# A two-layer streaming encoder on one core: early store of one residual block, accumulating last stores, four more weight blocks split by VectorE, and a longer lead for DMAs

## The chip, the cores and the metric

The kernel runs on one core of a Trainium2 chip, in one launch, and is timed in device microseconds (us). The engines work side by side: PE multiplies matrices, PEld loads its weights, DVE (VectorE) and ACT (ScalarE) work element by element, POOL (GpSimd) helps and issues DMAs, SP (SyncE) only issues DMAs. Each engine runs its own instructions in a fixed order and waits on semaphores. DMAs are issued by SP and ACT (hardware queues, with eight semaphore lanes DMAHW0 to DMAHW7 between them) and by POOL (software queue, lanes DMASW0 to DMASW7). An issue that reuses a lane waits, in its engine's order, until the lane's last DMA has landed. DMAs that add to what lies at their destination ("accumulating") are issued by POOL here.

## The reference

512 frames of 1024 features go through two layers, all in float32. Layer 0 is a convolution module and an MLP; layer 1 is latent attention and an MLP.

```python
def conformer_conv(h, w_pw1, b_pw1, w_dw, b_dw, ln_g, ln_b, w_pw2, b_pw2):
    u = h @ w_pw1 + b_pw1
    a, gate = jnp.split(u, 2, axis=-1)
    u = a * jax.nn.sigmoid(gate)
    ...  # 31 taps along time, each channel by itself, + b_dw
    u = jax.nn.silu(layer_norm(u, ln_g, ln_b))
    return u @ w_pw2 + b_pw2

def squared_relu_mlp(h, w1, w2):
    return jnp.square(jax.nn.relu(h @ w1)) @ w2

def reference(x, ...):
    h = x
    for layer in range(DEPTH):
        ...
        m = conformer_conv(...) if layer < N_A_LAYERS else mla_attention(...)
        h = h + rms_norm(m, mix_post_g[layer])
        f = squared_relu_mlp(rms_norm(h, ffn_pre_g[layer]), w_ff1[layer], w_ff2[layer])
        h = h + rms_norm(f, ffn_post_g[layer])
    return h
```

## The kernel before

**Products in three terms.** A float32 operand is kept as a higher part, which PE multiplies in one pass, and a lower part, the rest. A product is hi·hi + lo·hi + hi·lo, three matmuls (`products_of`, from line 772). A block of weights is 128 x 1024 numbers, 512 KB, and gives 24 matmuls of 512 columns. `weight` (731 to 766) fetches a block into a tile `raw` by SP and makes its parts `wh` and `wl` in one of two ways, decided by the condition in line 754:

- by `split` (789): ACT copies `raw` to `wh`, and VectorE subtracts, `wl = raw − wh`, each in two halves of 512 columns;
- or by DMA: ACT writes −`raw` rounded into `wl` and `raw` into `wh`, two copies each, and POOL issues an accumulating DMA of the whole block from DRAM onto `wl` (512 KB).

`lo_by_dma` (88) names the blocks that may go the second way; the blocks of `pw1`, the convolution's first product, are among them, save the first four (`i >= 4`).

**The convolution.** `pw1` has 16 blocks; column c of 8 (128 features) needs block c and its gate, block 8 + c. The blocks are used in pairs, so blocks 4 to 7 are those of columns c=2 and c=3. Columns 0, 1 and 3 have their 31 taps done by VectorE (`taps_vector`). Columns 2, 4, 5, 6 and 7 have them done by PE (`taps_tensor`, 1160) with 72 small matmuls of `uu` against tap weights that SP loads (`big<-cw`, 256 KB each). For these, `deal_tokens` (1151) sends the gated column through DRAM: ACT issues the store `dealt<-big` and four loads `uu<-dealt` of 64 KB. A layer norm follows, then `pw2` and the rest.

**The end.** `feed_forward(1, ...)` gives the last product by token block b = 0 to 3 (128 frames each) and half dh. `post_norm` (1063) calls `residual` (905) for each: ACT squares F and sums it into `stat`, VectorE multiplies F by a gain row. When both halves of a block are there, VectorE works out the scale rho in a chain of small operations on `stat`, and `finish` (1562) has VectorE add: h = F·rho + h. SP stores the first half, ACT the second, 256 KB each.

**What sets the order.** Nearly all instructions are recorded by `Program` and put in order by a planner in the kernel's own Python (`schedule`), which repeats its plan 16 times with new due times. PE's instructions keep the recorded order except for delays, and the planner puts filler matmuls (`mm<-ident`) where it expects PE to stand still. On the other engines the next instruction is the ready one with the earliest rank; a `dma_start` isn't placed earlier than `LEAD` nanoseconds ahead of its rank (line 251; used in 548). All instructions are issued in line 640, so the rows of the profile are told apart by the names of tiles: `raw`, `wh`, `wl` for weights, `big` and `tmp` for data and tap weights, `uu` and `dealt` for dealt columns, `mm` for PE's results, `h` for the residual stream, `row` for gains.

Of the kernel before, what the change touches and what calls it, by code (L numbers as in the profile page):

```python
# [11 lines left out]
ALU = mybir.AluOpType  # L12
# [10 lines left out]
DH = 512  # L23
# [64 lines left out]
def lo_by_dma(name):  # L88
    if name[0] == "ff1":
        return name[2] == 0 and name[3] < 4  # L90
    if name[0] == "ff2":
        return name[1] == 0 and name[2] == 3 and name[3] in LAST_BY_DMA
    return name[0] in ("pw1", "pw2")
# [152 lines left out]
GAIN_ON = ("vector",)  # L246
# [1 line left out]

PORT = ("tensor_tensor", "scalar_tensor_tensor")

LEAD = 16000.0

BESIDE = 3000.0

# [29 lines left out]
class Program:  # L284
# [166 lines left out]
    def schedule(self, tags):  # L451
# [71 lines left out]
        while left:  # L523
# [19 lines left out]
            while avail[e]:  # L543
# [3 lines left out]
                way = next(w for w in o.ways if w[0] == e)  # L547
                if way[1] == "dma_start" and o.rank > now + LEAD:

                    heappush(future[e], (o.rank - LEAD, o.n, o))  # L550
                    continue
# [92 lines left out]
def trunk(ctx: ExitStack, tc: tile.TileContext, xT, xN, wts, vec, along, rope, cw, out):  # L644
# [3 lines left out]
    nc = Program(tc.nc)  # L648
# [6 lines left out]
    def one(name, shape):  # L655
        return nc.tile(tag(name, 1, shape))
# [13 lines left out]
    def big(dt=F32):  # L670
        return nc.tile(BIG, dt)
# [24 lines left out]
    for k in range(KT):  # L696
        nc.sync.dma_start(out=xf[k], in_=xT[k])

    h = [one(f"h{b}", [P, D]) for b in range(TB)]
# [3 lines left out]
        out=ident, in_=ident, compare_op=ALU.not_equal, fill=1.0, base=0, pattern=[[-1, P]], channel_multiplier=1  # L703
# [13 lines left out]
    def scaled(name, src):  # L717

        lo, hi = ([big(F32R) for _ in range(2)] for _ in range(2))
        for o in range(2):  # L720
            raw = big()
            nc.sync.dma_start(out=raw, in_=src[:, o * T : (o + 1) * T])
            g0 = VEC[GAINS[name[0]]] + 4 * o
            gain = vt[:, g0 : g0 + 4].rearrange("p (k o) -> p k o", o=1).to_broadcast([P, 4, P])
            nc.vector.tensor_tensor(
                out=raw.rearrange("p (k m) -> p k m", m=P), in0=raw.rearrange("p (k m) -> p k m", m=P), in1=gain, op=ALU.mult
            )
            split(raw, slice(0, T), (hi[o], lo[o]))
        return hi, lo

    def weight(key):

        while key not in blocks:
            name, parts = USE[len(blocks)]
            i, n = BLK[parts[0][0]], _cols[BLK[parts[0][0]]]
            if name[0] in GAINS:
                blocks[name] = scaled(name, wts[i])
                continue
            raw, hi, lo = nc.tile(RAW), nc.tile(WH, F32R), nc.tile(WL, F32R)
            step = 256 if i < 2 else n  # L740
            for o in range(0, n, step):
                nc.sync.dma_start(out=raw[:, o : o + step], in_=wts[i, :, o : o + step])
            for other, sign in parts[1:]:
                if sign > 0:
                    nc.gpsimd.dma_start(out=raw, in_=wts[BLK[other]], accum_op=ALU.add)
                else:
                    second = nc.tile(RAW)
                    nc.sync.dma_start(out=second, in_=wts[BLK[other]])
                    for o in range(0, n, 512):
                        nc.vector.tensor_tensor(  # L750
                            out=raw[:, o : o + 512], in0=raw[:, o : o + 512], in1=second[:, o : o + 512], op=ALU.subtract
                        )
            src = raw if len(parts) > 1 else wts[i]
            if i >= 4 and lo_by_dma(name):

                for o in range(0, n, 512):
                    for dst, scale in ((lo, -1.0), (hi, 1.0)):
                        nc.scalar.activation(dst[:, o : o + 512], raw[:, o : o + 512], AF.Copy, scale=scale)
                nc.gpsimd.dma_start(out=lo, in_=src, accum_op=ALU.add)
            else:  # L760
                step = 256 if i < 2 else min(n, 512)
                engines = VG if name[0] in ATT else ("vector",)
                for o in range(0, n, step):
                    split(raw, slice(o, o + step), (hi, lo), engines=engines)
            blocks[name] = hi, lo
        return blocks[key]
# [22 lines left out]
    def split(src, s, dst, d=None, engines=("vector",)):  # L789

        d = s if d is None else d
        nc.scalar.activation(dst[0][:, d], src[:, s], AF.Copy)
        nc.binary(engines, out=dst[1][:, d], in0=src[:, s], in1=dst[0][:, d].bitcast(F32), op=ALU.subtract)
# [77 lines left out]
    def row(name):  # L871
        t = nc.tile(ROW)
        nc.early = 30000.0
        nc.sync.dma_start(out=t, in_=along[ROWS.index(name)])
        nc.early = 0.0
        return t
# [28 lines left out]
    def residual(F, g, b, dh, o, st, on, r2):  # L905


        nc.scalar.activation(
            JUNK, F[b][dh], AF.Square, scale=1.0 / 32 if r2 is None else r2[:, b : b + 1], accum_out=st[:, o : o + 1]
        )  # L910
        nc.binary(on, out=F[b][dh], in0=F[b][dh], in1=g[:, dh * DH : (dh + 1) * DH], op=ALU.mult)

    def rms(st, nb=2, factor=None):

        var = st[:, :nb]
        ss = st[:, 16 : 16 + 2 * nb].rearrange("p (b d) -> p b d", d=2)
        nc.vector.scalar_tensor_tensor(
            out=var, in0=ss[:, :, 0], scalar=RMS_EPS, in1=ss[:, :, 1], op0=ALU.add, op1=ALU.add
        )
        return rsqrt_tiny(st, var, nb, factor)  # L920

    def add_norm(F, rho, bs):

        for i, b in enumerate(bs):
            for dh in range(2):
                cs = slice(dh * DH, (dh + 1) * DH)
                nc.vector.scalar_tensor_tensor(
                    out=h[b][:, cs], in0=F[b][dh], scalar=rho[:, i : i + 1], in1=h[b][:, cs], op0=ALU.mult, op1=ALU.add
                )
                yield b, cs  # L930
# [30 lines left out]
    def feed_forward(layer, X, F):  # L961
# [6 lines left out]
        for q in range(4):  # L968
# [29 lines left out]
            def sides(q, p):  # L998
                return [weight(("ff2", layer, q, p, u)) for u in range(2)]
# [60 lines left out]
                                    op=ALU.add if dests[to] > 0 else ALU.subtract,  # L1060
                                )

    def post_norm(gen, F, g, then, groups, r2=None, last=False):

        group = {b: bs for bs in groups for b in bs}
        seen, st = dict.fromkeys(groups, 0), {}
        for b, dh in gen:
            bs = group[b]
            if not seen[bs]:
                st[bs] = nc.tile(STAT)  # L1070
            if last:

                nc.early = (4000.0, 4000.0, 0.0, 0.0)[b]
            residual(F, g, b, dh, 16 + 2 * (b - bs[0]) + dh, st[bs], GAIN_ON, r2)
            seen[bs] += 1
            if seen[bs] == 2 * len(bs):
                then(bs, rms(st[bs], len(bs), None if r2 is None else r2[:, bs[0] : bs[-1] + 1]))
            nc.early = 0.0

    PAIRS = HALVES[HA], HALVES[HB]  # L1080
    SINGLES = tuple((b,) for b in range(TB))
# [161 lines left out]
    acc, last = big(), LN_ORDER[-1]  # L1243
# [15 lines left out]
    for t0, n in (HA, HB):  # L1259
# [3 lines left out]
        st = nc.tile(STAT)  # L1263
# [5 lines left out]
            out=var, in0=sm[:, nb : 2 * nb], scalar=LN_EPS, in1=d2, op0=ALU.add, op1=ALU.subtract  # L1269
# [20 lines left out]
    def mixer_out(layer, gen):  # L1290

        MF, r2 = token_blocks(), one(f"r2_{layer}", [P, TB])
        Xn = [pair() for _ in range(KT)]

        def on_half(t):
            y, bs = prenorm(Xn, f"ffn_pre{layer}", t), HALVES[t]
            nc.vector.scalar_tensor_tensor(
                out=r2[:, bs[0] : bs[1] + 1], in0=y, scalar=1.0 / 32, in1=y, op0=ALU.mult, op1=ALU.mult
            )

        post_norm(gen(MF), MF, row(f"mix_post{layer}"), by_halves(MF, on_half), PAIRS)
        return Xn, r2

    Xn, r2 = mixer_out(0, pw2)
# [4 lines left out]
    F, r1 = [[None, None] for _ in range(TB)], big()  # L1309
# [4 lines left out]
    def on_half(t):  # L1314
        r1t[t] = prenorm(XH, None, t, r1)

        for b in HALVES[t]:
            nc.sync.dma_start(out=order.rearrange("(m r) d -> r m d", r=R)[b], in_=h[b])

    post_norm(feed_forward(0, Xn, F), F, row("ffn_post0"), by_halves(F, on_half), PAIRS, r2)  # L1320


# [5 lines left out]
    def undealt(a, t):  # L1328

        r0 = t[0] // M  # L1330
        return natural(a)[:, r0 : r0 + t[1] // M]
# [82 lines left out]
    for t in (HA, HB):  # L1414
# [4 lines left out]
        for j in range(2):  # L1419
            rows = slice(64 * j, 64 * j + 64)  # L1420
            nc.vector.tensor_tensor(
                out=undealt(KL[j][rows], t), in0=kr[rows], in1=undealt(KR[rows], t).bitcast(F32), op=ALU.subtract
# [8 lines left out]
    st = nc.tile(STAT)  # L1431
# [127 lines left out]
    Xn, r2 = mixer_out(1, wo)  # L1559
    F = [[None, None] for _ in range(TB)]  # L1560

    def finish(bs, rho):
        for b, cs in add_norm(F, rho, bs):
            (nc.sync, nc.scalar)[cs.start > 0].dma_start(out=out[b, :, cs], in_=h[b][:, cs])

    post_norm(feed_forward(1, Xn, F), F, row("ffn_post1"), finish, SINGLES, r2, last=True)

    with tc.manual_schedule():
        nc.run(tags)
# [126 lines left out]
```

## Time and profile before

| | us |
|---|---|
| median of 3 runs (lowest, highest) | 1066.44 (1065.2, 1067.63) |
| the profiled execution | 1068.46 |
| its span, first to last instruction | 1066.7 |
| mean granted clock of PE, as a share of full speed | 0.993 |
| POOL busy | 141.6 (13%) |
| DMA, share of 16 engines: hardware queue q1, software queue q0 | 40.9%, 25.6% |

Rows of a timeline give start, length, engine, operation, output and inputs, how many instructions are drawn together, and in brackets the idle time of the engine before them and what ended it. ACTq and SPq are DMA issues of these engines. Rows of a tile's view give the issue time of its DMAs and, in a row of its own, how long after the issue they landed. A window gives the busy time of each engine in a stretch, in the order PE, PEld, DVE, ACT, POOL, then the granted clock, the share of time that the DMA engines were busy, and GB/s. A group's row gives the count, the busy time and the mean length of one in ns, and then idle time.

### The profile page before, as it was taken

The page shows a single profiled execution, that of the slowest core. Times are in us where ns is not written, and L with a number is a line of the kernel's source. Part 1 is how long each engine was busy: PE and PEld are TensorE (multiplying, and loading weights), DVE is VectorE, ACT ScalarE, POOL GpSimd, SP SyncE. Part 2 cuts the span into 40 slices and gives each one's busy share as a digit, 9 for nine tenths or more (in the row PEclk, how much of TensorE's full clock was granted, in tenths as well). Part 3 has the DMA queues.
Part 4 walks back from the last instruction along what each step waited for, and adds up shares of the span by engine and source line. Part 5 has one row for each costly group of instructions (what it writes and reads, how often), then busy time and mean ns, then how long its engine had stood idle before and what let it go on. Part 6 is the DMA issues. An engine that isn't in the chain of part 4 may idle for free. (4 is left out here: it accounts for less than half of the span.)

```text
span 1066.7 us, 15181 instructions
## 1 busy us (share of the span) xinstructions
PE 1045.5 (98%) x5284; PEld 884.7 (83%) x5284; DVE 764.1 (72%) x1559; ACT 640.9 (60%) x1343; POOL 141.6 (13%) x165
## 2 busy tenths in 40 slices
PE   8989999999999999999999999999999999999996
PEld 7878988988888888888888888889888888888885
DVE  6497994857438737959988987547574495497698
ACT  8543497766545446545767877558565554454652
POOL 1110011100100100001104533301010010000010
PEclk9989999999999999999999999999999999999998
DMA  9995888657866848658923132557599388485684
GB/s 288 300 254 171 287 211 236 156 168 207 253 171 190 257 126 241 189 182 227 237 69 93 56 100 81 174 182 179 161 245 253 112 235 257 143 243 168 187 237 129
DMA packets 67613, 204.08 MB, mean 191 GB/s; under 512 B 7632, under 2 KB 13904, under 8 KB 67536
## 3 DMA queue, kind: packets, MB, share of 16 engines
q1 hardware_dynamic: 49680, 150.15, 40.9%
q0 software_dynamic: 13536, 49.29, 25.6%
q10 hardware_dynamic: 4320, 3.68, 1.1%
q8 instruction: 41, 0.67, 0.3%
q14 instruction: 36, 0.29, 0.1%
HBM read 197.58 MB, written 5.51 MB: 190 GB/s over the span
## 5 line engine op out<-in xcount | busy, mean ns | idle before, releaser
L640 PE MATMUL mm<-big,wh 128*128 128x512 f32 (+1 forms) x1512 | 441.1, 374 | 1.2 <-ACT wh L640 1.2
L640 PE MATMUL mm<-wh,big 128*128 128x512 f32 (+1 forms) x1216 | 374.7, 387 | 0.0
L640 ACT ACTIVATE wh<-raw 128x512 fp32r<-128x512 f32 (+2 forms) x444 | 251.0, 612 | 117.7 <-PE mm L640 73.8
L640 PEld LDWEIGHTS mm<-big,wh 128*128 128x128 f32 x1512 | 275.6, 188 | 52.4 <-ACT wh L640 1.5
L640 DVE TENSOR_TENSOR wl<-raw,wh 128x512 fp32r<-128x512 f32 (+1 forms) x356 | 227.7, 680 | 106.5 <-ACT wh L640 104.1
L640 PE MATMUL mm<-big,wl 128*128 128x512 f32 (+1 forms) x756 | 282.5, 374 | 0.0
L640 PEld LDWEIGHTS mm<-wh,big 128*128 128x128 f32 x1216 | 226.3, 188 | 46.9
L640 PE MATMUL mm<-wl,big 128*128 128x512 f32 (+1 forms) x608 | 234.9, 387 | 0.1
L640 PEld LDWEIGHTS mm<-big,wl 128*128 128x128 f32 x756 | 142.6, 189 | 25.7 <-DVE wl L640 0.5
L640 PEld LDWEIGHTS mm<-wl,big 128*128 128x128 f32 x608 | 114.2, 188 | 23.4 <-DVE wl L640 0.2
L640 POOL DMA_DIRECT2D raw<-wts x64 | 55.5, 867 | 572.7 <-DMA raw<-wts 190.4
L640 ACT ACTIVATE big<-tmp 128x256 f32<-128x256 f32 (+1 forms) x208 | 95.9, 493 | 43.2 <-DVE tmp L640 37.3
L640 DVE TENSOR_TENSOR big<-big,big 128x512 f32<-128x512 f32 (+4 forms) x103 | 69.8, 698 | 55.9 <-ACT big L640 55.6
L640 ACT ACTIVATE tmp<-mm 128x512 f32<-128x512 f32 (+1 forms) x75 | 41.7, 556 | 103.1 <-PE mm L640 102.0
L640 PE MATMUL mm<-big,big 128*128 128x256 f32 (+3 forms) x520 | 83.5, 310 | 1.8 <-DVE big L640 1.8
L640 PEld LDWEIGHTS mm<-big,big 128*128 128x128 f32 x520 | 73.1, 189 | 7.0 <-DVE big L640 2.3
L640 ACT ACTIVATE big<-mm 128x512 f32<-128x512 f32 (+5 forms) x106 | 56.6, 537 | 33.9 <-PE mm L640 32.9
L640 DVE TENSOR_TENSOR big<-tmp,big 128x512 fp32r<-128x512 f32 (+1 forms) x96 | 60.9, 642 | 15.3 <-ACT big L640 12.7
L640 DVE SCALAR_TENSOR_TENSOR big<-big,vt,big 128x512 fp32r<-128x512 f32 (+29 forms) x95 | 63.3, 736 | 8.0 <-ACT big L640 8.0
L640 DVE TENSOR_TENSOR big<-big,mm 128x512 f32<-128x512 f32 x96 | 63.7, 683 | 3.2 <-PE mm L640 2.8
L640 DVE TENSOR_TENSOR tmp<-big,big 128x512 f32<-128x512 f32 x80 | 53.3, 686 | 8.9 <-ACT big L640 8.9
L640 POOL DMA_DIRECT2D wl<-wts x30 | 26.1, 869 | 213.0 <-ACT wl L640 113.3
(90 smaller groups left out, 775.9 us busy)
## 6 DMA issues: line engine op xcount, KB each, us to landing
raw<-wts SPq DMA_DIRECT2D x222, 512.0 KB, 5.0
raw<-wts POOLq DMA_DIRECT2D x64, 512.0 KB, 7.9
wl<-wts POOLq DMA_DIRECT2D x30, 512.0 KB, 8.4
big<-cw SPq DMA_DIRECT2D x45, 256.0 KB, 5.6
big<-wts SPq DMA_DIRECT2D x12, 256.0 KB, 4.3
row<-along SPq DMA_DIRECT2D x5, 512.0 KB, 5.5
raw<-wts SPq DMA_DIRECT2D x12, 192.0 KB, 2.7
big<-xT SPq DMA_DIRECT2D x8, 256.0 KB, 4.2
```

Source lines behind the costliest of these rows:

```text
L640: return f(*args, **kwargs)
```

## The change

```diff
-LEAD = 16000.0
+LEAD = 20000.0
...
-            if i >= 4 and lo_by_dma(name):
+            if i >= 8 and lo_by_dma(name):
...
-        nc.binary(on, out=F[b][dh], in0=F[b][dh], in1=g[:, dh * DH : (dh + 1) * DH], op=ALU.mult)
+        if g is not None:
+            nc.binary(on, out=F[b][dh], in0=F[b][dh], in1=g[:, dh * DH : (dh + 1) * DH], op=ALU.mult)
...
-    def post_norm(gen, F, g, then, groups, r2=None, last=False):
+    def post_norm(gen, F, g, then, groups, r2=None, last=()):
...
-            residual(F, g, b, dh, 16 + 2 * (b - bs[0]) + dh, st[bs], GAIN_ON, r2)
+            residual(F, None if b in last else g, b, dh, 16 + 2 * (b - bs[0]) + dh, st[bs], GAIN_ON, r2)
...
+    AHEAD = (2,)
+    grow = row("ffn_post1")
+    for b in AHEAD:
+        nc.sync.dma_start(out=out[b], in_=h[b])
+
     def finish(bs, rho):
-        for b, cs in add_norm(F, rho, bs):
-            (nc.sync, nc.scalar)[cs.start > 0].dma_start(out=out[b, :, cs], in_=h[b][:, cs])
-
-    post_norm(feed_forward(1, Xn, F), F, row("ffn_post1"), finish, SINGLES, r2, last=True)
+        for b in bs:
+            if b not in AHEAD:
+                for _, cs in add_norm(F, rho, bs):
+                    (nc.sync, nc.scalar)[cs.start > 0].dma_start(out=out[b, :, cs], in_=h[b][:, cs])
+                continue
+            for dh in range(2):
+                cs = slice(dh * DH, (dh + 1) * DH)
+                nc.vector.scalar_tensor_tensor(
+                    out=h[b][:, cs], in0=F[b][dh], scalar=rho[:, 0:1], in1=grow[:, cs], op0=ALU.mult, op1=ALU.mult
+                )
+                nc.gpsimd.dma_start(out=out[b, :, cs], in_=h[b][:, cs], accum_op=ALU.add)
+
+    post_norm(feed_forward(1, Xn, F), F, grow, finish, SINGLES, r2, last=AHEAD)
```

Four more blocks of `pw1` (4 to 7, columns c=2 and c=3) get their lower part from VectorE: four accumulating DMAs of POOL and eight ACT copies go, eight VectorE subtractions come. For token block 2 the residual stream before its last addition is stored to the output by SP (512 KB), VectorE makes F·rho·gain in one instruction per half, without the multiply in `residual`, and POOL adds that to the output in DRAM by two accumulating DMAs of 256 KB. A DMA may be planned up to 20 us ahead of its rank instead of 16.

The planner orders the whole program anew. PE's order differs in about its first fifth and in the attention, and ahead of the taps of column c=7 it has four filler rows (`mm<-ident`) where it had one. The places below are those that matter for what follows.

The first is on ACT, at the dealing of column c=2: `dealt` is the store of the gated column to DRAM, `uu` the four loads back, and the brackets name the semaphores waited for. Before:

```order
L640 DMA dealt_529<-big_518 128x512 [waits DMAHW0_49,DVE_49]
L640 ACTIVATE wl_532<-raw_484 128x512 [waits DMAHW2_49,DMASW0_49]
L640 ACTIVATE wl_532<-raw_484 128x512
L640 ACTIVATE wh_547<-raw_484 128x512 [waits PE_49]
...
L640 ACTIVATE wh_598<-raw_544 128x512 [waits PE_49]
L640 DMA uu_109<-dealt_529 32x4x128 [waits DMAHW3_49,DMAHW0_49]
L640 DMA uu_109<-dealt_529 32x4x128 [waits DMAHW5_49]
L640 DMA uu_109<-dealt_529 32x4x128 [waits DMAHW7_49]
L640 DMA uu_109<-dealt_529 32x4x128 [waits DMAHW1_49]
L640 ACTIVATE wh_598<-raw_544 128x512
```

And now:

```order
L640 ACTIVATE wh_508<-raw_457 128x512 [waits PE_49]
L640 ACTIVATE wh_508<-raw_457 128x512
...
L640 DMA dealt_545<-big_536 128x512 [waits DMAHW2_49,DVE_49]
L640 ACTIVATE wl_581<-raw_516 128x512 [waits DMAHW6_49]
L640 ACTIVATE wl_581<-raw_516 128x512
L640 ACTIVATE wh_591<-raw_516 128x512 [waits PE_49]
L640 ACTIVATE wh_591<-raw_516 128x512
L640 DMA uu_109<-dealt_545 32x4x128 [waits DMAHW7_49,DMAHW2_49]
L640 DMA uu_109<-dealt_545 32x4x128 [waits DMAHW1_49]
L640 DMA uu_109<-dealt_545 32x4x128 [waits DMAHW3_49]
L640 DMA uu_109<-dealt_545 32x4x128 [waits DMAHW5_49]
```

The store now waits for lane 2 instead of lane 0 and stands behind the two weight copies that it stood ahead of; the loads wait for lanes 7, 1, 3 and 5, where the last waited for lane 1.

The second is SP's queue at the same place; it shows which loads hold those lanes (`raw` are weight blocks, `big` from `cw` tap weights). Before:

```order
L640 DMA raw_603<-wts 128x1024 [waits DMAHW5_49,Activation_49]
L640 DMA raw_646<-wts 128x1024 [waits DMAHW6_49,Activation_49]
L640 DMA raw_686<-wts 128x1024 [waits DMAHW7_49,Activation_49]
L640 DMA raw_736<-wts 128x1024 [waits DMAHW1_49,Activation_49]
L640 DMA big_849<-cw 128x512 [waits DMAHW2_49]
L640 DMA big_856<-cw 128x512 [waits DMAHW4_49]
L640 DMA big_863<-cw 128x512 [waits DMAHW6_49]
L640 DMA big_872<-cw 128x512 [waits DMAHW0_49]
```

And now:

```order
L640 DMA raw_570<-wts 128x1024 [waits DMAHW5_49,DVE_49]
L640 DMA raw_623<-wts 128x1024 [waits DMAHW6_49,Activation_49]
L640 DMA raw_665<-wts 128x1024 [waits DMAHW7_49,Activation_49]
L640 DMA raw_724<-wts 128x1024 [waits DMAHW0_49,Activation_49]
L640 DMA big_806<-cw 128x512 [waits DMAHW1_49]
L640 DMA big_815<-cw 128x512 [waits DMAHW3_49]
L640 DMA big_826<-cw 128x512 [waits DMAHW4_49]
L640 DMA big_833<-cw 128x512 [waits DMAHW5_49]
```

The rows stand at the same eight places of the queue. Lane 1, on which the last `uu` load waited, was held by the fourth of them; lane 5, on which it waits now, is held by the eighth, the fourth load of tap weights.

The third is VectorE's end: the last sum of F, the rest of the statistics, and the products that are stored (`row` is the gain, `big` holds F, `stat` the statistics, the lower number block 2's, the higher block 3's). Before:

```order
L640 TENSOR_TENSOR big_8149<-big_8149,mm_10408 128x512 [waits PE_49]
L640 TENSOR_TENSOR stat_10502<-stat_10502 128x1 [waits DVE_49]
L640 TENSOR_TENSOR big_8133<-big_8133,row_10035 128x512
...
L640 TENSOR_TENSOR big_8149<-big_8149,row_10035 128x512
...
L640 SCALAR_TENSOR_TENSOR h_1452<-big_8133,stat_10502,h_1452 128x512
...
L640 SCALAR_TENSOR_TENSOR h_1452<-big_8280,stat_10502,h_1452 128x512
...
L640 SCALAR_TENSOR_TENSOR h_1456<-big_8149,stat_10520,h_1456 128x512 [waits DVE_49]
L640 SCALAR_TENSOR_TENSOR h_1456<-big_8297,stat_10520,h_1456 128x512
```

And now:

```order
L640 TENSOR_TENSOR big_8150<-big_8150,mm_10404 128x512 [waits PE_49]
L640 TENSOR_TENSOR stat_10499<-stat_10499 128x1 [waits DVE_49]
...
L640 TENSOR_TENSOR big_8150<-big_8150,row_9998 128x512
L640 SCALAR_TENSOR_TENSOR stat_10517<-stat_10517 128x1 [waits DVE_49]
L640 SCALAR_TENSOR_TENSOR h_1337<-big_8278,stat_10499,row_9998 128x512 [waits DMAHW6_49]
...
L640 SCALAR_TENSOR_TENSOR h_1337<-big_8134,stat_10499,row_9998 128x512
...
L640 SCALAR_TENSOR_TENSOR h_1339<-big_8150,stat_10517,h_1339 128x512 [waits DVE_49]
L640 SCALAR_TENSOR_TENSOR h_1339<-big_8295,stat_10517,h_1339 128x512
```

One multiply of block 2 by the gain stood between the last sum and the statistics and is gone; block 2's products take the gain row instead of h, wait for the lane of the early store, and come in the other order of halves.

## The prediction

> **What bounds the kernel now.** I read the page first, then PE's waits, then PE's timeline at the longest of them, then the transfers behind that wait.
>
> ```profile
> span 1066.7 us, 15181 instructions
> PE 1045.5 (98%) x5284; PEld 884.7 (83%) x5284; DVE 764.1 (72%) x1559; ACT 640.9 (60%) x1343; POOL 141.6 (13%) x165
> PE mm L640 <- DMA uu<-dealt: 3.7, 1, 3.7
> ```
>
> PE is busy for 1045.5 of 1066.7 us, so an edit on another engine gains only where PE stands still (21.2 us in all) or runs slowly. The largest single wait is for `uu`, the dealt input of the first convolution column that PE computes itself (c=2). PE's timeline there, and its windows (length, PE busy, granted clock, DMA share, GB/s):
>
> ```profile
> 67.30 11.04 PE L640 MATMUL mm<-uu,big 128*128 128x128 f32 x72 [3.69 <-DMA uu<-dealt]
> ...
> 107.78 8.20 PE L640 MATMUL mm<-uu,big 128*128 128x128 f32 x72
> ```
>
> ```profile
> 68.00:70.00 2.00, 2.00 (x12) 0.50 0.84 156
> 70.00:72.00 2.00, 2.00 (x11) 0.50 1.02 237
> 72.00:74.00 2.00, 2.00 (x15) 0.73 1.09 248
> ```
>
> The 72 tap matmuls of c=2 start 3.69 us late, and then take 11.04 us where those of the next such column take 8.20: 2.84 us more. The windows say why: the clock is 0.50 from 68 to 72 and comes back within the next window. One late transfer costs 3.69 + 2.84 = **6.53 us**. Without it PE would start these taps at 67.30 − 3.69 = 63.61.
>
> Why `uu` is late stands in the transfers' tiles (issue, then landing) and in ACT's timeline, since ACT issues these DMAs:
>
> ```profile
> L640 SPq DMA_DIRECT2D big<-cw x1: 328/328/328, 33.9 to 33.9; - x1
> DMA to landing us min/median/max: 15.2/15.2/15.2
> ```
>
> ```profile
> 49.18 0.33 ACTq L640 DMA_DIRECT2D dealt<-big  x1
> 55.99 6.52 ACTq L640 DMA_DIRECT2D uu<-dealt  x4
> ```
>
> ```profile
> L640 SPq DMA_DIRECT2D raw<-wts x1: 328/328/328, 51.8 to 51.8; - x1
> DMA to landing us min/median/max: 10.3/10.3/10.3
> ```
>
> ```profile
> L640 ACTq DMA_DIRECT2D uu<-dealt x1: 310/310/310, 62.2 to 62.2; - x1
> DMA to landing us min/median/max: 5.0/5.0/5.0
> ```
>
> The store `dealt<-big` waits for a semaphore lane that a load of tap weights holds: issued at 33.9, landed at 33.9 + 15.2 = 49.1, and the store goes at 49.18. Of the four `uu` loads the last waits for the lane of a `raw` load, 51.8 + 10.3 = 62.1; it goes at 62.2, lands at 67.2, and PE starts at 67.30. Such long landings are a backlog, as the DMA view of the first 60 us and a window inside it show (packets, MB, share of 16 engines):
>
> ```profile
> q1 hardware_dynamic: 5801, 13.11, 61.3%
> q0 software_dynamic: 1072, 3.93, 35.2%
> ```
>
> ```profile
> 45.00:50.00 5.00, 5.00 (x23) 4.10 (x22) 4.39 (x7) 0.42 (x2) 0.00 (x0) 1.00 0.99 354
> ```
>
> The accumulating DMAs are the dear part: 35.2% of 60 us is 21.1 us of all engines for 3.93 MB, 5.37 us per MB; a plain transfer takes 36.8 us for 13.11 MB, 2.81 per MB. One accumulate of 512 KB (0.524 MB) is 2.8 us, one plain load of that size 1.5.
>
> **The change part by part.**
>
> *Four first blocks by VectorE.* The accumulates that go are the first four that POOL issues, and eight VectorE subtracts come in for eight ScalarE copies:
>
> ```profile
> 17.42 1.01 POOL L640 DMA_DIRECT2D wl<-wts  x1 [15.40 <-ACT wl L640]
> ...
> 26.15 0.86 POOL L640 DMA_DIRECT2D wl<-wts  x1 [1.22 <-ACT wl L640]
> ```
>
> ```profile
> L640 DVE TENSOR_TENSOR wl<-raw,wh 128x512 fp32r<-128x512 f32 x347 | 223.9, 687 | 106.4 <-ACT wh L640 104.1 <-PE mm L640 1.6
> ```
>
> ```profile
> 20.00:25.00 5.00, 5.00 (x31) 4.37 (x30) 2.42 (x11) 3.13 (x7) 1.73 (x2) 1.00 1.01 205
> 25.00:30.00 5.00, 5.00 (x25) 4.19 (x25) 1.29 (x2) 3.94 (x8) 0.86 (x1) 1.00 1.05 283
> ```
>
> ACT, with 60% busy no bound, loses eight copies, POOL four issues, and DVE gains 8 × 0.687 = 5.5 us. They fall between about 17 and 30 us, where DVE is busy 2.42 and 1.29 of 5 us, so that 2.58 + 3.71 = 6.3 us are free in those two windows alone: cost 0. If that cover were gone, up to 5.5 us of DVE would delay the first gated columns.
>
> The DMA queues lose 4 × 2.8 = 11.2 us of work ahead of `dealt` and `uu`, by the share of queue q0; by the price of a plain transfer of as many bytes, the lower bound, it would be 4 × 1.5 = 6.0. I take the first, which is measured on these very transfers. Against this stands the new order of SP's queue, shown above. The last `uu` load now waits for lane DMAHW5, whose holder is the tap-weight load four places further down SP's queue than the `raw` load it waits for today. The load at that place in the trace of before:
>
> ```profile
> L640 SPq DMA_DIRECT2D big<-cw x1: 495/495/495, 56.1 to 56.1; - x1
> DMA to landing us min/median/max: 10.9/10.9/10.9
> ```
>
> It landed at 56.1 + 10.9 = 67.0. With nothing drained, `uu` would be complete at 67.0 + 5.0 = 72.0 against 67.2 now. The backlog must shrink by 4.8 us for the change to break even here, and by 72.0 − 63.61 = 8.4 us for the stall to vanish. With 11.2 `uu` is complete at 60.8, which is 2.8 us in time; with 6.0 it is complete at 66.0, and 2.4 us of the wait stay. I take the whole stall as gone: **−3.69**, and with it the slow clock, **−2.84**.
>
> The Trainium skill, "TensorE: Matmul & The Clock Gate", Part 1: The HAM clock gate, says that the array falls to half rate after an idle window of about 3.4 us and comes back after about 3.4 us of sustained work, by a window that runs freely. An estimate from that page is 3.4 / 2 = 1.7 us of loss instead of 2.84, and the sum below would be 1.1 us smaller; the trace holds the half clock for longer than that, and the trace's 2.84 stands.
>
> What is late next? The engines that feed the later columns have room to follow PE forward. DVE's timeline in the last columns:
>
> ```profile
> 94.96 0.69 DVE L640 TENSOR_TENSOR tmp<-mm,big 128x512 f32<-128x512 f32 x1 [2.22 <-PE mm L640]
> ```
>
> ```profile
> 135.86 0.39 PE L640 MATMUL mm<-ident 128*128 128x128 f32 x2
> 136.09 8.20 PE L640 MATMUL mm<-uu,big 128*128 128x128 f32 x72
> ```
>
> DVE waits 2.22 us for PE there, so it moves forward with it, and the layer norm behind it too. The order has three more filler rows ahead of the taps of the last column (four for one). The one of before takes 136.09 − 135.86 = 0.23 us, so the three cost **+0.7** (0 if PE would have waited there).
>
> *The longer lead and the new plan.* The planner may place DMAs up to 20 us ahead instead of 16, and orders everything anew; PE's own order differs in the first fifth and in the attention. PE has no other wait of DMA in before, so I take 0, and ±1.5 for small waits that come and go.
>
> *The third block's early store.* 512 KB go on SP's queue ahead of the last weight load: 0.524 × 2.81 = 1.5 us of DMA. PE has no wait in the list of its waits that goes back to such a load, so there is some slack behind it. I take 0, with 0 and +1.5 as ends.
>
> *The tail.* Two DVE multiplies by the gain go, the last addition leaves DVE, and POOL issues two accumulating stores of 256 KB. DVE's and ACT's rows of before, the last store, and the only kind of accumulate that the trace has at a quiet time (512 KB into on-chip memory):
>
> ```profile
> 1057.79 0.69 DVE L640 TENSOR_TENSOR big<-big,row 128x512 f32<-128x512 f32 x1
> ...
> 1062.21 1.41 DVE L640 SCALAR_TENSOR_TENSOR h<-big,stat,h 128x512 f32<-128x512 f32 x2
> ```
>
> ```profile
> 1058.53 0.19 ACT L640 ACTIVATION_READ_ACCUMULATOR junk<-big,r 128x1 f32 x1
> ```
>
> ```profile
> L640 SPq DMA_DIRECT2D out<-h x1: 332/332/332, 1063.7 to 1063.7; - x1
> DMA to landing us min/median/max: 2.1/2.1/2.1
> ```
>
> ```profile
> L640 POOL DMA_DIRECT2D raw<-wts x1: 862/862/862, 217.3 to 217.3; - x1
> DMA to landing us min/median/max: 5.4/5.4/5.4
> ```
>
> One removed multiply lies at 1057.79, ahead of the square that ends at 1058.72 and that block 3's statistics wait for; the other lies before PE's end. So DVE still ends at about 1063.6, and block 3's last store lands at 1063.7 + 2.1 = 1065.8 as now. By the new order block 2's products end some 2.7 and 2.0 us before DVE's end, at about 1060.9 and 1061.6. POOL issues in 0.86, so the second goes at 1061.7. An accumulating store to DRAM isn't in this trace. From below it takes as long as the plain store, 2.1: 1063.8, hidden. From above the second alone takes 5.4: 1067.1, +1.3. I take both together as one accumulate of 512 KB, since they have its bytes and run side by side: 1060.9 + 5.4 = 1066.3, **+0.5**.
>
> The Trainium skill, "DMA: Bandwidth & Descriptors", Anatomy of one DMA, gives about 2.0 us plus the bytes at 436 GB/s for a transfer that GpSimd issues. The estimate by that page is 2.6 us for 256 KB, and the tail's term would be 0; the quiet 512 KB accumulate of the trace took 5.4 against its 3.2, so the trace doesn't agree for accumulates.
>
> Sum: −3.69 − 2.84 + 0.7 + 0.5 = **−5.3 us**. The profiled execution took 1068.46 us (span 1066.7), 2.0 above the median of 1066.44; it becomes 1063.1 with a span of 1061.4, and the median becomes 1066.44 − 5.3 = **1061.1**. Its own range is 1058 to 1064.
>
> **The rivals.**
>
> *The wait only shrinks, or moves.* The margin of 2.8 us is thin against landings of 10 to 15 us, and the lower price of an accumulate leaves a wait of 2.4. With that wait, or one of its size at the taps of the last column, and without the slow clock: −5.3 + 2.4 = −2.9, so 1063.5. For it speaks the lane four places further back; against it that the removed transfers all lie ahead of what `uu` waits for, and that q0's share is measured.
>
> *No change.* The executions without the profiler may have no such stall (they are 2 us faster than the profiled one), or the slow start of DVE's layer norm gives the gain back: 1066.
>
> *Slower.* The mechanism is the lane. If the earlier DMAs that the longer lead admits fill the queues as fast as the accumulates leave them, none of the relief reaches this place, `uu` is complete at up to 72.0 instead of 67.2, and the time is 1066.4 + 4.8 = 1071. It decides from a relief of less than 4.8 on. Against it: SP's loads up to that place are the same in number, so their bytes do not grow.
>
> **How the numbers follow.** The forecast has 0.64, the part gain 0.14, no change 0.11, slower 0.11. About 0.2% (2.1 us, 1064.3 here) is what a measurement tells from no change. Of the part gain two thirds lie below it: faster 0.64 + 0.09 = 0.73; same 0.05 + 0.11 = 0.16; slower 0.11. The range reaches from 1057.5 (all terms at their good ends, no fillers, no tail, the order at −1.5, give 1058.4; the other 0.9 is within what three runs spread, 1065.2 to 1067.63) to 1067.5, which takes in the part gain, no change and both upper ends of the unknown costs; slower is left out.
>
> **What would show it right or wrong.** Right: no PE wait for `uu`, clock 1.00 from 60 to 80, 72 taps of c=2 in 8.2 us beginning near 63.6, the fourth `uu` load issued before 58. Wrong: that load issued after 62, a new wait of PE in the taps or the layer norm, DVE full at 20 to 30 us with PE idle, or `out<-h` of POOL landing more than 1.3 us behind SP's last store.

## The result and the profile after

| | before | changed |
|---|---|---|
| median, us (lowest to highest; 4 runs each) | 1065.82 (1063.93 to 1067.63) | 1072.57 (1071.87 to 1073.7) |
| ratio, with its 95% interval | | 1.0069 (1.0052 to 1.0086) |
| profiled execution, us | 1068.46 | 1071.87 |
| its span | 1066.7 | 1070.1 |

The changed kernel is slower by 0.7%, where the prediction was 0.5% faster. Two lines of its page, and the list of PE's waits in full:

```profile
span 1070.1 us, 15177 instructions
PE 1045.1 (98%) x5284; PEld 882.6 (82%) x5284; DVE 771.8 (72%) x1563; ACT 637.9 (60%) x1335; POOL 142.3 (13%) x165
```

```profile
PE mm L640 <- DVE big L640: 2.9, 4, 1.4
PE bc L640 <- DVE big L640: 2.0, 3, 1.2
PE mm L640 <- POOL big L640: 1.6, 1, 1.6
PE mm L640 <- ACT wh L640: 1.2, 1, 1.2
PE mm L640 <- DVE wl L640: 1.1, 2, 0.7
PE bc L640 <- DVE stat L640: 0.4, 1, 0.4
```

The wait for `uu` is gone from the list, as predicted; the waits for DVE have grown (1.8 and 1.5 us in the first profile of before). The place where the gain was expected, on PE's timeline, ACT's timeline, in the tile of the last `uu` load and in the DMA view of the first 60 us:

```profile
64.20 8.20 PE L640 MATMUL mm<-uu,big 128*128 128x128 f32 x72
```

```profile
45.88 0.34 ACTq L640 DMA_DIRECT2D dealt<-big  x1
52.13 4.37 ACTq L640 DMA_DIRECT2D uu<-dealt  x4
```

```profile
L640 ACTq DMA_DIRECT2D uu<-dealt x1: 310/310/310, 56.2 to 56.2; - x1
DMA to landing us min/median/max: 4.9/4.9/4.9
```

```profile
q1 hardware_dynamic: 7017, 15.33, 72.4%
q0 software_dynamic: 576, 2.10, 18.6%
```

The software queue moved half as much (2.10 MB, before 3.93), the last `uu` load went at 56.2 and landed at 61.1 (forecast 60.8), and the 72 taps start at 64.20 without a wait and take 8.20 us. That part came as written down.

The end of the program did not. POOL's timeline, the tiles of its second accumulating store and of SP's last plain store, and the windows behind them (length, busy time of PE, PEld, DVE, ACT and POOL, clock, DMA share, GB/s):

```profile
1058.53 1.77 POOL L640 DMA_DIRECT2D out<-h  x2 [18.16 <-DVE stat L640]
```

```profile
L640 POOL DMA_DIRECT2D out<-h x2: 872/957/1042, 1058.5 to 1059.3; - x2
DMA to landing us min/median/max: 4.0/5.1/6.3
```

```profile
L640 SPq DMA_DIRECT2D out<-h x1: 333/333/333, 1061.0 to 1061.0; - x1
DMA to landing us min/median/max: 4.9/4.9/4.9
```

```profile
1064.00:1065.00 1.00, 0.00 (x0) 0.00 (x0) 0.00 (x0) 0.00 (x0) 0.00 (x0) 0.50 0.82 270
1065.00:1066.00 1.00, 0.00 (x0) 0.00 (x0) 0.00 (x0) 0.00 (x0) 0.00 (x0) 0.50 0.02 6
1066.00:1068.00 2.00, 0.00 (x0) 0.00 (x0) 0.00 (x0) 0.00 (x0) 0.00 (x0) 0.50 0.00 0
1068.00:1070.00 2.00, 0.00 (x0) 0.00 (x0) 0.00 (x0) 0.00 (x0) 0.00 (x0) 0.50 0.00 0
```

All DMAs have landed by 1065.9 (1061.0 + 4.9), and then the span goes on for 4.2 us in which nothing works. The trace itself, below the page's views, has one record there: a DRAIN of POOL, its closing instruction, which starts with POOL's last DMA issue at 1059.24, lasts 10.10 us and ends at 1069.34. The kernel before has it too: from 1042.44 to 1053.49, 11.05 us, behind its last accumulating load, long ahead of its end.

To see where the rest went, I counted PE's matmuls without the fillers and compared the start of the same one in each trace. The reference is a second profile of the kernel before (e7 below), in us; a minus is ahead of it:

| start of matmul | there at | first profile of before | changed | e1 | e4 | e9 | e11 |
|---|---|---|---|---|---|---|---|
| 900th, behind the layer norm | 169.44 | +4.75 | −2.38 | +0.55 | −2.22 | −1.62 | −1.36 |
| 2500th, attention begins | 510.72 | +4.75 | −1.40 | +0.55 | +0.40 | −1.00 | −0.80 |
| 3900th, attention has ended | 743.04 | +4.92 | +1.96 | +0.54 | +4.39 | −1.02 | −0.86 |
| last | 1051.76 | +4.93 | +2.27 | +1.45 | +5.24 | −0.42 | −0.67 |
| from the last to the span's end | 10.0 | 10.0 | 16.1 | 16.9 | 10.0 | 10.0 | 16.8 |

So the changed kernel gains 2.4 us in the front, loses 4.7 between 170 us and PE's end, most of it in the attention, and loses 6.1 behind PE's end. That adds up to 8.4 us, against one execution that at 1063.54 us lay below its median; by the ratio of the times it is 7.3. And the execution profiled first of the kernel before was not a typical one.

### The profile page after: what moved, and what is told of

It reads as the page before. It is cut to its first block, busy times and chain, and to the rows that moved or that the text cites. A ratio compares the mean times of both kernels' runs of the same rounds, so it can differ in the third digit from the quotient of the medians.

```text
span 1070.1 us, 15177 instructions
## 1 busy us (share of the span) xinstructions
PE 1045.1 (98%) x5284; PEld 882.6 (82%) x5284; DVE 771.8 (72%) x1563; ACT 637.9 (60%) x1335; POOL 142.3 (13%) x165
## 4 chain that ended last, share of the span: by engine, by line
PE 87%; DVE 9%; ACT 3%; issue 1%; DMA 0%; DVEq 0%; ACTq 0%
PE mm L640 84%; DVE big L640 5%; PE bc L640 2%; ACT big L640 2%; DVE stat L640 2%; DVE wl L640 1%; DVE h L640 0%; ACT wh L640 0%; DVE tmp L640 0%; DMA vt<-vec 0%; ACT junk L640 0%; ACT tmp L640 0%; DVEq L1709 0%; DVE wq L640 0%; DVEq L640 0%
## 5 line engine op out<-in xcount | busy, mean ns | idle before, releaser
L640 DVE TENSOR_TENSOR wl<-raw,wh 128x512 fp32r<-128x512 f32 (+1 forms) x360 | 233.0, 683 | 156.6 <-ACT wh L640 151.7
L640 DVE TENSOR_TENSOR big<-tmp,big 128x512 fp32r<-128x512 f32 (+1 forms) x96 | 60.8, 640 | 11.0 <-ACT big L640 8.9
L640 POOL DMA_DIRECT2D wl<-wts x26 | 23.0, 885 | 218.4 <-ACT wl L640 122.6
```

What stands on the lines that cost most here:

```text
L640: return f(*args, **kwargs)
```

## The experiments

The ratios are to the kernel before, timed on the same chip in turn with the run; its medians there were 1064.4 to 1064.9.

**e1, the tail alone.** The changed kernel with two lines undone:

```diff
-LEAD = 20000.0
+LEAD = 16000.0
-            if i >= 8 and lo_by_dma(name):
+            if i >= 4 and lo_by_dma(name):
```

> Of the three edits only the tail: block 2's early store and its two accumulating stores by POOL; the lead is 16 us and blocks 4 to 7 have their lower parts by DMA as before. PE's order is that of before (over 99%). Theory A (POOL's closing instruction, which starts when POOL has issued its last DMA and lasted 11.05 us in before and 10.10 us in the changed kernel, sets the end): it ends about 10 us after the issue at about 1061.9, so the span is about 1072.5 and the time +6 us on before, about 1.006. Theory B (the accumulating stores themselves are slow and hold up the last plain stores: landing 4.0 to 6.3 us instead of 2.1): the last landing is near 1068.5, the span 1069.5, the time +2.5 to +3 us, about 1.0025. Theory C (the loss is all in the re-planned attention): no change, 0.999 to 1.001.

Measured: 1072.19 us, ratio 1.0068 (1.0049 to 1.0088). Theory A; B's 1.0025 and C's no change lie outside the interval. PE's last matmul starts at 1053.21, POOL's DRAIN runs from 1059.07 to 1069.08, and the span ends at 1070.1. The tail alone makes a kernel as slow as the whole change.

**e2, two plain stores by POOL.** The kernel before, with

```diff
-            (nc.sync, nc.scalar)[cs.start > 0].dma_start(out=out[b, :, cs], in_=h[b][:, cs])
+            (nc.gpsimd if b == 2 else (nc.sync, nc.scalar)[cs.start > 0]).dma_start(
+                out=out[b, :, cs], in_=h[b][:, cs])
```

> The kernel before with one edit: block 2's two last stores are issued by POOL as plain DMAs, with no accumulation and no early store. Theory A in its first form (POOL's closing instruction lasts about 10 us from the last issue, whatever the DMA does): the span is about 1073, the time +6 us, 1.006. Theory A in a second form (it ends 3.7 to 3.9 us after POOL's last DMA has landed, as 1049.6 to 1053.5 in before and 1065.6 to 1069.3 in the changed kernel): with a landing of about 3 us at 1065.2 it ends at 1069, the time +3 us, 1.003. Theory B (accumulation is what is slow): within 0.5 us of before, 0.9995 to 1.0005.

Measured: 1068.26 us, 1.0031 (1.0020 to 1.0042): theory A in its second form. Nothing is accumulated and nothing else is moved, and yet 3 us are lost. The tile of POOL's stores:

```profile
L640 POOL DMA_DIRECT2D out<-h x2: 568/572/576, 1058.2 to 1058.9; - x2
DMA to landing us min/median/max: 2.4/2.6/2.8
```

The second lands at 1058.88 + 2.8 = 1061.7, and the DRAIN ends at 1065.63. In all traces its end follows the last landing of POOL's DMAs, not their issue:

| trace | POOL's last DMA issued | landed | DRAIN ends | after the landing |
|---|---|---|---|---|
| before | 1042.47 | 1049.6 | 1053.49 | 3.9 |
| changed | 1059.26 | 1065.5 | 1069.34 | 3.8 |
| e1 | 1059.09 | 1065.1 | 1069.08 | 4.0 |
| e2 | 1058.88 | 1061.7 | 1065.63 | 4.0 |
| e3 | 1050.07 | 1055.7 | 1059.53 | 3.8 |
| e4 | 1042.54 | 1049.8 | 1053.55 | 3.7 |
| e11 | 1056.97 | 1063.3 | 1067.06 | 3.8 |

The span ends 0.8 to 1.0 us behind the DRAIN where that is last (e1, e2, changed, e11), and about as long behind the last plain store's landing elsewhere. Between e1 and e2 the accumulating store lands 6.0 us after its issue and the plain one 2.8. So the tail's price has two parts: about 3.3 us for the closing instruction, and about as much again for the longer landing of an accumulate. The Trainium skill, "DMA: Bandwidth & Descriptors", Anatomy of one DMA, gives about 2.0 us plus the bytes at 436 GB/s for a DMA from GpSimd, an estimate of 2.6 us for 256 KB: the plain stores with 2.4 and 2.8 agree, the accumulating ones with 4.0 and 6.3 don't.

**e3, block 0 in block 2's place.** `AHEAD = (0,)` in the changed kernel.

> The changed kernel with block 0 in the place of block 2 for the early store and the accumulating stores; PE's order is that of the changed kernel. POOL's last issue then lies near 1047, some 12 us ahead of the end. Theory A: POOL's closing instruction ends near 1057 and hides; the span ends about 0.9 us behind the last plain store, 6 us shorter than that of the changed kernel: about 1064, a time of 1066 to 1067, level with before (0.999 to 1.002). Theory B: the accumulates no longer meet the last stores, a gain of 2.8 us only: 1069.5 to 1070, 1.003 to 1.004. Theory C: as the changed kernel, 1072.5, 1.006 to 1.007.

Measured: 1068.18 us, 1.0032 (1.0019 to 1.0045). The ratio is that of theory B, but the trace is not: the DRAIN ends at 1059.53 and the span 10.2 us behind the last matmul, as before, which is what A says. It is PE that is late: its last matmul starts at 1057.62, 3.6 us behind the changed kernel, though PE's order differs in a few rows only; VectorE's matches to 96%. This made the order of the rest the next suspect.

**e4, no tail.** The kernel before with `LEAD = 20000.0` and `i >= 8`.

> The changed kernel without its tail edit: lower parts of blocks 4 to 7 by VectorE and the lead of 20 us stay, all last stores are plain. Theory A: 6 us less than the changed kernel, 1066 to 1067, 0.999 to 1.002, with PE's last matmul near 1054.5 as there. Theory B: 1069.5 to 1070, 1.003 to 1.004. Theory C: 1072, 1.006. In all of them PE doesn't wait for uu at 64 us, and the attention (500 to 740 us) holds about 3 us more of PE's waits than before if the lead or the blocks are what changed its order.

Measured: 1069.09 us, 1.0045 (1.0028 to 1.0061). A miss for all three: the tail is that of before (10.0 us behind the last matmul), and the time is worse than A allows. By the table PE is 2.2 us ahead behind the layer norm and 4.4 behind after the attention.

**e5 to e8: the parts of that, and before once more.** e5 is the kernel before with `i >= 8` alone, e6 with `LEAD = 20000.0` alone, e7 is the kernel before, and e8 is e5 with

```diff
-                if way[1] == "dma_start" and o.rank > now + LEAD:
+                lead = 20000.0 if now < 200000.0 else LEAD
+                if way[1] == "dma_start" and o.rank > now + lead:
...
-                    heappush(future[e], (o.rank - LEAD, o.n, o))
+                    heappush(future[e], (o.rank - lead, o.n, o))
```

> Of the three edits only the lower parts of blocks 4 to 7 by VectorE; lead 16 us, plain last stores. Theory D (the removed accumulates empty the queues, uu lands before PE wants it, and PE is some 4 us ahead at 280 us of where e1 and e2 have it with the order of before; what the attention then loses comes from the lead): PE's last matmul near 1049 to 1051, time 1061 to 1063, 0.996 to 0.999. Theory E (any new plan gives 3 to 7 us back in the attention, since VectorE is busy 19 of 20 us there and the order that before has is the good one): the gain is there at 280 us and gone at 740 us; 1064 to 1069, 1.000 to 1.0045.

> Of the three edits only the longer lead, 20 us. Theory D: the accumulates stay, so the front gains nothing against e1 (within 1 us at 280 us), and the attention loses about 3 to 5 us, as in the changed kernel: PE's last matmul near 1057, time 1067 to 1069, 1.003 to 1.0045. Theory E: the attention loses as well, in the same size; it differs from D only in e5. If the lead alone costs nothing (0.999 to 1.001), neither the lead nor the accumulates, but the two together make the loss of e4.

> The kernel before once more, for a second profile of it. If the execution profiled first was an unusually slow one (1068.46 us against a median of 1064.4 of 23 runs since): no or a short wait for uu (under 1 us), the clock whole from 66 to 74 us, PE's last matmul near 1053, the span near 1063. If the stall of 3.69 us belongs to every execution: PE's last matmul near 1056.7, the span near 1066.7, and e1 and e2, in which PE did not wait there, differ by something that their edits do.

> Lower parts of blocks 4 to 7 by VectorE, plain last stores, and the lead of 20 us only while the planner's clock is under 200 us, 16 us after it. Theory D: the gain of about 4 us in the front stays and the attention loses at most 1 us: time 1060 to 1062, 0.996 to 0.998. Theory E: the attention's order is new here too (it matches that of before by 91 to 96% on PE and by 73% on VectorE in the worst tenth), and takes 3 to 7 us back: 1064 to 1068, 1.000 to 1.003.

| | median, us | ratio (interval) |
|---|---|---|
| e5, blocks alone | 1067.19 | 1.0024 (1.0014 to 1.0033) |
| e6, lead alone | 1068.39 | 1.0039 (1.0025 to 1.0052) |
| e7, before | 1064.39 | 0.9999 (0.9983 to 1.0015) |
| e8, blocks, lead in front only | 1065.92 | 1.0006 (0.9997 to 1.0015) |

The times of e5, e6 and e8 are those of theory E: each is a new plan, and none is faster. Of E's course e8 has both halves: it is ahead by 2.87 us at the 900th matmul and back at +0.22 when the attention ends. e5 doesn't have the first half, and neither does e6 (+0.63 and +3.59 at the 900th matmul). In e5 the last `uu` load lands at 61.8 and PE is 1.5 us ahead at the last column's taps; it loses that in the layer norm, where PE waits 1.06 and 0.93 us and the clock is at half for 3.4 us. In the profiled execution of e6 the last `uu` load goes at 63.3 and lands at 66.9, and PE meets the stall again (the row names DVE, but the landing came last, 0.2 us before PE's start):

```profile
67.10 9.62 PE L640 MATMUL mm<-uu,big 128*128 128x128 f32 x72 [3.28 <-DVE big L640]
```

e7 settled what the first profile was. PE's and ACT's timelines, PE's windows at the same place (length, PE busy, clock, DMA share, GB/s), and two rows of PE's waits:

```profile
65.28 8.28 PE L640 MATMUL mm<-uu,big 128*128 128x128 f32 x72 [0.21 <-issue]
```

```profile
47.62 0.33 ACTq L640 DMA_DIRECT2D dealt<-big  x1
53.78 6.24 ACTq L640 DMA_DIRECT2D uu<-dealt  x4
```

```profile
68.00:70.00 2.00, 2.00 (x20) 1.00 1.01 254
70.00:72.00 2.00, 2.00 (x20) 1.00 1.08 246
```

```profile
PE mm L640 <- DVE big L640: 1.7, 3, 0.7
PE bc L640 <- DVE big L640: 1.6, 3, 0.7
```

The same program waits 0.21 us for `uu` here, not 3.69, and the clock stays whole: the last load goes at 59.7 instead of 62.2. How often the stall comes is not shown. Of 92 executions of the kernel before in these experiments 57 have a mean clock of PE of 0.997 or more (median 1064.06 us) and 35 have 0.996 or less (1066.4), none as little as the first profile's 0.993, and a half clock of some 6.8 us is worth 0.003. But the mean doesn't say where the clock was low: e2, e5 and e10 have a half clock of 3.4 us at 143 us, in the layer norm, with no stall at `uu`.

**e9 and e10: the two halves exchanged.** Both pin the order and the choice of engine by a table of operation numbers, with the planner's own dependences untouched; each engine's operations take their turn from the table. The core, in `schedule` and in a new `pin`:

```diff
+        for e in [e for e in ENGINES for _ in range(2)]:
...
+                op.ways = [w for w in op.ways if w[0] == e]
+                op.choose(op.ways[0])
+                if last is not None:
+                    last.then, op.led = op, 1
+                last = op
...
-            op.left, op.at, op.done, op.held, op.skips = op.npreds, 0.0, False, 0.0, 0
+            op.left, op.at, op.done, op.held, op.skips = op.npreds + op.led, 0.0, False, 0.0, 0
...
+            if op.then is not None:
+                op.then.left -= 1
+                if not op.then.left:
+                    later(op.then, max(op.then.at, now))
```

e9 is e4 with its own order for the first 200 us and that of before from there; e10 is the kernel before with its own order for the first 200 us and that of e4 from there.

> e4 (lower parts of blocks 4 to 7 by VectorE, lead of 20 us, plain last stores) with the order of its first 200 us on every engine, and from there on, on every engine, the order and the choice of engines that the kernel before has. Theory E (the front's gain of 3.6 us is real and the new order of the attention loses it): PE is 3 to 4 us ahead of the second profile of before from 280 us to the end, no further loss between 500 and 740 us, the time 1060.5 to 1061.5, 0.996 to 0.998. Theory F (PE ahead of its data loses it whatever the order, since VectorE and the loads bound the attention): the lead is gone by 740 us, the time 1064 to 1066, 0.9995 to 1.0015.

> The kernel before (lower parts of blocks 4 to 7 by DMA, plain last stores) with its own order for the first 200 us, and from there on, on every engine, the order and the choice of engines of e4. Theory E: level with before at 280 us, 5 to 8 us behind it at the end (e4 went from 3.4 ahead at 280 us to 5.2 behind at the end), the time 1070 to 1072, 1.005 to 1.007. Theory F: no loss of its own in that order: 1064 to 1066, 0.9995 to 1.0015.

Measured: e9 1063.0 us, 0.9983 (0.9972 to 0.9994); e10 1074.36 us, 1.0089 (1.0071 to 1.0107). The order decides, as theory E has it: with the old one PE keeps its lead through the attention (table: −1.00 to −1.02), and e10, with the new one, is 0.7 us behind at the 900th matmul and 11.1 at the last. The sizes are not E's. e9 had 1.6 us to keep and not 3 to 4 (e4 has 2.2 at that place, not the 3.4 and 3.6 of the two expectations), so its time lies between the ranges of E and F; and e10 loses more than E said. PE's waits of e9, then of e10 (L666 is the line of the same helper):

```profile
PE mm L666 <- DVE big L666: 1.7, 3, 0.8
PE bc L666 <- DVE big L666: 1.1, 3, 0.6
```

```profile
PE mm L666 <- DVE big L666: 4.1, 7, 1.3
PE mm L666 <- ACT wh L666: 3.4, 3, 1.2
PE bc L666 <- DVE big L666: 2.7, 5, 0.8
```

e9 is faster than both kernels, by 0.17% on before. Its 12 executions all have a mean clock of 0.997 and lie between 1061.34 and 1064.51 us.

**e11, the whole change with the old order behind 200 us**, pinned in the same way (that order from e1, which has the tail).

> The changed kernel with all three edits and its own order for the first 200 us, and from there on, on every engine, the order and the choice of engines of e1 (which are those of before, with the changed tail). Theory G (the three terms add: front, order of the rest, tail): e9 took 0.9983 of before, and the tail costs 6 to 7 us, so 1069 to 1071, 1.004 to 1.005, about 2 to 4 us faster than the changed kernel; PE's last matmul near 1051.5, the span's end 16 to 17 us behind it. Rival (the tail's price shrinks when PE ends earlier, or the tail's DMAs disturb the old order): under 1067, 1.002, or level with the changed kernel, 1.0065 to 1.007.

Measured: 1068.97 us, 1.0032 (1.0018 to 1.0046), just under theory G's range; PE's last matmul (1051.09) and the span's end 16.8 us behind it are as it says. Against e9 (medians of `before` 1064.9 and 1064.8) the tail costs 6.0 us; against the changed kernel's 1.0069 the old order gives back 0.0037, 3.9 us, which the two intervals leave open by some 2 us either way.

## Why the prediction was wrong

*The front: the queues did as written, the price was wrong.* The accumulates removed did empty the queues: `uu` landed at 61.1 against 60.8 forecast, and at 61.8 with the blocks alone (e5), where it landed at 66.9 with the lead alone (e6) and at 65.2 in e7. The three fillers cost 0.89 − 0.22 = 0.67 us (before the last column's taps, 129.96 to 130.85 in the changed kernel and 131.09 to 131.31 in e7) against 0.7. The failed step is the price, −3.69 − 2.84, taken from the profiled execution. That sum treats the execution as typical, and it was 2.0 us over the median that stood beside it; the second profile has 0.21 of the 3.69 and none of the 2.84. The rival "no change" named this, at a chance of 0.11.

Of the 2.4 us that the changed kernel is ahead of e7 at the 900th matmul, the taps of c=2 bring only 0.45. 0.70 is there by the twentieth matmul, where the two profiles of before, one program, are 1.46 apart; the fillers take 0.67 back; and 1.9 come in the layer norm, for which the prediction had no term. PE's rows there in e7, then in the changed kernel:

```profile
141.16 0.83 PE L640 MATMUL bc<-col,big 128*128 128x128 f32 x4 [0.75 <-DVE big L640]
142.65 0.71 PE L640 MATMUL bc<-col,tmp 128*128 128x128 f32 x4 [0.66 <-ACT tmp L640]
```

```profile
138.89 1.69 PE L640 MATMUL bc<-col,big 128*128 128x128 f32 x12
140.53 0.71 PE L640 MATMUL bc<-col,tmp 128*128 128x128 f32 x4
```

These two waits are there with the blocks alone and with the lead alone (e5, e6), and gone in every kernel that has both in the front (changed, e3, e4, e8, e9, e11); why it takes both was not tried. With the rest in its old order the front is worth 1.8 us by the times (e9, 0.6 to 3.0 by its interval).

*"PE has no other wait of DMA in before, so I take 0, and ±1.5" for the new plan.* This failed: 4.7 us by the trace, 3.9 by e11 against the changed kernel. The rows of PE's timeline in the attention of the changed kernel, then the largest of e7 there:

```profile
537.23 0.98 PE L640 MATMUL mm<-big,big 128*128 128x256 f32 x6 [1.35 <-DVE big L640]
550.98 2.42 PE L640 MATMUL mm<-big,big 128*128 128x256 f32 x18 [1.10 <-DVE big L640]
...
602.74 0.44 PE L640 MATMUL bc<-ident,big 128*128 128x128 f32 x2 [1.18 <-DVE big L640]
```

```profile
537.76 1.58 PE L640 MATMUL mm<-big,big 128*128 128x256 f32 x11 [0.73 <-DVE big L640]
```

Waits for DVE had a row in the list before (1.8 us in three), and they are what grew. The six new plans without a pinned order (changed, e3, e4, e5, e6, e8) lose 1.9 to 7.5 us from the 900th matmul to the last; the traces with the order of before (both profiles of it, e1, e2, e9, e11) lose 1.2 at most against e7. So the planned order of before is worth some microseconds that its neighbours lack, and the prediction's 0 with ±1.5, drawn from the waits for DMA alone, had no room for losing them. Waits explain some 2.9 of the 4.7 us (in the attention PE stands still for 6.5 us in the changed kernel and 3.6 in e7); for the rest PE shows as busy throughout (1 us of it between the layer norm and the attention), and what slowed it there stays open. That the loss goes with the order and not with the blocks or the lead is shown by e9 and e10; what in the order does it, row for row, was not tried.

*The tail, +0.5 with +1.3 as its upper end.* It failed: +6.1 by the trace, 6.0 by e11 against e9. The landing that I bounded by 5.4 us was 6.3, a small miss, and SP's last plain store beside it took 4.9 instead of 2.1. The large one is that I ended the program at the last landing. POOL's closing instruction ends 3.8 us later. The trace of before has it too, below the page's views; it cost nothing there because POOL's last DMA was issued 24 us ahead of the end. The two steps beside it were right: VectorE ended 6.9 us behind the last matmul's start as before (6.9), and PE stood busy throughout from 1000 to 1050 us, so the early store held up no reader.

*The rival on the slower side* had the wrong mechanism: the lane was no obstacle, and its chance of 0.11 was a chance for something else.

## What to carry to other kernels

A DMA issued by GpSimd near the end is paid until its landing plus GpSimd's closing instruction, about 3.8 us more. Leave the last stores to the hardware queues; an accumulating store that is issued early enough costs nothing at the end (in e3, with the last issue at 1050 us, the span ended 10.2 us behind PE's last matmul, as before). Where a planner orders the program anew, its new order is a term of the sum with a sign of its own: pin the old order behind the edit and see what the edit is worth by itself. And before a stall is sold as a gain, ask by a second profile, and by the spread of the executions, whether other executions have it.

## What the runs showed of the hardware

An accumulating store of 256 KB to DRAM landed 4.0 to 6.3 us after its issue where a plain one by the same engine took 2.4 to 2.8 (e2), and the plain store that SP issued beside it took 4.9 instead of 2.1. POOL's closing DRAIN ended 3.7 to 4.0 us after the landing of POOL's last DMA in seven traces, plain or accumulating, at a busy time (1049.6) and at a quiet one. And one program, with nothing changed, may or may not run into a stall whose margin is a fraction of a microsecond (0.21 us in e7, 3.69 in the first profile): once PE stood for 3.69 us, the clock was at half for about 6.8 us. In e6 a wait of 3.28 us was followed by 3.4 us of half clock, and 72 taps that take 8.20 us at full clock took 9.62. In e2, e5 and e10 the clock fell to half for 3.4 us in the layer norm, behind two waits of 0.5 to 1.1 us, while in e1 waits of 1.13 and 0.66 us at the same place left it whole.
